# Spreading the token scales inside the second column pair of each SwiGLU stage, and other PSUM pools for that pair's tiles

## The chip, the cores and the metric

The kernel runs on one core of a Trainium2 chip. The metric is the device time of one launch in microseconds (us). Engines are called as in the profile: PE (TensorE matmul), PEld (its weight load), DVE (VectorE), ACT (ScalarE), POOL (GpSimd), SP (SyncE, which issues most transfers).

## What is computed

A decoder trunk of two layers over 512 tokens of width 1024, in float32. Each layer runs a half-step SwiGLU, a token mixer, a second half-step SwiGLU and a gated per-layer embedding. There are thus four SwiGLU stages, with a hidden width of 2816:

```python
def rms_norm(x, g, eps=NORM_EPS):
    y = x32 * lax.rsqrt(jnp.mean(x32 * x32, axis=-1, keepdims=True) + eps)
    return (y * g.astype(f32)).astype(x.dtype)
...
def swiglu(h, wg, wu, wd):
    return (jax.nn.silu(h @ wg) * (h @ wu)) @ wd
...
h = h + 0.5 * swiglu(rms_norm(h, norm_ffn_a[i]), ffn_a_wg[i], ffn_a_wu[i], ffn_a_wd[i])
```

## The kernel before

The activations stand transposed: eight tiles of 128 features by 512 tokens. A float32 product is made of three matmuls, since each operand is held as a high part and a remainder: `mm3` (L310) issues them. A weight block is loaded by SP, its high part is copied by ACT (L174) and the remainder is taken by DVE (L176). Such a pair is a piece; five slots hold pieces (`NHL`, L66), and `used` (L187) gives slots back and calls `pump`, which loads and splits what comes next.

The norm's gain is folded in before the matmul (`prep`, L350), but the scale of each token, 1/rms, is not: it is multiplied in later. `norm_stats` (L392) gets it: PE sums the squares into one column per token block (`token_rms`, L329), DVE makes the reciprocal root in eleven short instructions (L318 to L324), and `spread` (L333) turns the column into a full tile `Rt`: DVE puts it on a diagonal (L339), PE multiplies that with ones into the PSUM tile `rbc` (L344), DVE copies it out (L348).

`ffn` (L440) runs a list of steps. The hidden columns are taken in pairs of 128-column blocks. The first pair is computed plainly (`plain`, L444): for f = 0 and 1, 24 matmuls into a gate tile G (PSUM pool A) and 24 into an up tile U (pool B). Inside it stand `norm_stats` (L455), the building of four groups of combined inputs (`right`, L366, whose last instruction is DVE L382), and the plain pair's end, L459 to L463: gate times scale on DVE, Silu on ACT, up times gate on DVE, the high part on ACT, the remainder on DVE. Every other pair (`pair`, L465) uses a seven-product scheme: products in the order 0, 3, 4, 1, 5, 2, 6, each of 24 matmuls, gathered in three PSUM tiles X (pool A), Y (pool B) and Z (pool C). Products 3 to 6 read what `right` builds; product 0 and the plain products don't need L382. Product 2 goes to Z, the others to X and Y. L490, L492 and L495 copy partial sums out; L497, L499 and L501 put quarters of the result into O; product 6 goes on adding to X, so it follows L499. O shares its SBUF range with the scratch V of `right`.

PSUM has eight banks: pools A to D with two buffers each (L45). Pool C has no user in the plain pair. The order of instructions is not as written: the framework traces the program, then orders each engine's queue by program-order priority in a model of the run; each engine works its queue in order. A PSUM buffer is handed on when the last reader of its tile has run.

The four stages are called here a0, b0, a1, b1: first and second SwiGLU of layer 0, then of layer 1. `pair` for j = 1 follows `plain` at once and j = 2 follows that; the `down` steps (L514) come in from there.

Of the kernel before, what the change touches and what calls it, by code (L numbers as in the profile page):

```python
# [15 lines left out]
ALU = mybir.AluOpType  # L16
# [22 lines left out]
def trunk(ctx, tc, a, stop=None):  # L39
    nc = tc.nc  # L40
# [6 lines left out]
    def bank(tag, name="ps"):  # L47
        return psum.tile([P, NT], F32, tag=tag, name=name)
# [23 lines left out]
    O = fr[:, 0:2048].rearrange("p (f u n) -> p f u n", f=2, u=2)  # L72
    V = fr[:, 0:2048].rearrange("p (s n) -> p s n", s=8)
    aeb = [fr[:, 2048 + i * NT : 2048 + (i + 1) * NT] for i in range(3)]
    Rt = fr[:, 3584:4096]
# [9 lines left out]
    def sc(name="sc"):  # L85
        at = sc_at[scs[0] % (4 if wide[0] else 2)]
        scs[0] += 1
        return fr[:, at : at + NT]
# [98 lines left out]
    def used(*ps):  # L187
        for p in ps:
            hl_order.append(p.slot)
        pump()  # L190
# [27 lines left out]
    def done(u):  # L218
        used(*u.pieces)
# [90 lines left out]
    def mm3(ps, lh, ll, rh, rl, first, last):  # L310
        nc.tensor.matmul(ps, lh, rh, start=first, stop=False)  # L311
        nc.tensor.matmul(ps, lh, rl, start=False, stop=False)  # L312
        nc.tensor.matmul(ps, ll, rh, start=False, stop=last)  # L313
# [12 lines left out]
    def token_rms(sq, dim, eps, rcol):  # L326
        ps = bank("D", "ssum")
        for b in range(NB):
            nc.tensor.matmul(ps[:, b : b + 1], sq[:, b * P : (b + 1) * P], ones[:, 0:1],  # L329
                             start=True, stop=True)  # L330
        rsqrt_cols(rcol, ps[:, :NB], dim, eps, NB)

    def spread(rcol, dst, act=False):  # L333
        dg = sc("diag")
        if act:
            for b in range(NB):
                nc.scalar.activation(dg[:, b * P : (b + 1) * P], ident, AF.Copy, scale=rcol[:, b : b + 1])
        else:
            nc.vector.tensor_tensor(  # L339
            dg.rearrange("p (b n) -> p b n", n=P),  # L340
            ident[:, None, :].to_broadcast([P, NB, P]),
            rcol[:, :, None].to_broadcast([P, NB, P]), op=ALU.mult)
        ps = bank("D", "rbc")
        nc.tensor.matmul(ps, ones, dg, start=True, stop=True)  # L344
        if act:
            nc.scalar.activation(dst, ps, AF.Copy)
        else:
            nc.vector.tensor_copy(dst, ps)  # L348
# [43 lines left out]
    def norm_stats(want_row=True):  # L392
        rcol = small.tile([P, NB], F32, tag="rcol", name="rcol", bufs=2)
        token_rms(acc, DM, 1e-6, rcol)
        if not want_row:
            return rcol, None
        spread(rcol, Rt)
        return rcol, Rt
# [41 lines left out]
    def ffn(steps, me, nxt, side=None):  # L440

        state = {}

        def plain(ps):  # L444
            for f in range(2):
                G, U = bank("A", "G"), bank("B", "U")
                for c in range(KD):
                    w = [ps[2 * f + c % 2].part(s).rearrange("p (i n) -> p i n", i=4)[:, c // 2, :]
                         for s in range(2)]
                    for u, t in enumerate((G, U)):  # L450
                        us = slice(u * P, (u + 1) * P)
                        mm3(t, w[0][:, us], w[1][:, us], *plain_x[c], c == 0, c == KD - 1)
                used(*ps[2 * f : 2 * f + 2])
                if f == 0:
                    state["R"] = norm_stats()[1]  # L455
                for i in (2 * f, 2 * f + 1):
                    right(i, *me)
                g, u = (O[:, 1, k, :] for k in range(2)) if f else aeb[:2]
                nc.vector.tensor_tensor(g, G, state["R"], op=ALU.mult)  # L459
                nc.scalar.activation(g, g, AF.Silu)  # L460
                nc.vector.tensor_tensor(u, U, g, op=ALU.mult)
                nc.scalar.activation(hid[f], u, AF.Copy)
                nc.vector.tensor_tensor(hid[6 + f], u, hid[f].bitcast(F32), op=ALU.subtract)  # L463

        def pair(j, ps):  # L465
            X, Y, Z = bank("A", "X"), bank("B", "Y"), bank("C", "Z")
            k = [0]

            def product(op, out, start):
                p = ps[k[0]]  # L470
                k[0] += 1
                w = [p.part(s).rearrange("p (i n) -> p i n", i=4) for s in range(2)]
                for u in range(2):
                    o, us = out[:, u * 256 : (u + 1) * 256], slice(u * P, (u + 1) * P)
                    for i in range(4):
                        for n, (lw, r) in enumerate(((0, 0), (0, 1), (1, 0))):
                            nc.tensor.matmul(o, w[lw][:, i, us], xr[:, r, op, i, :],  # L477
                                             start=start and u == 0 and i == 0 and n == 0,
                                             stop=i == 3 and n == 2, skip_group_check=True)
                used(p)  # L480

            def quarter(f, t):
                return O[:, f, :, 256 * t : 256 * t + 256]

            def q2(t):
                return t.rearrange("p (u n) -> p u n", u=2)

            pa, pe, pb = aeb
            product(0, X, True)
            nc.scalar.activation(pa, X, AF.Copy, scale=-1.0)  # L490
            product(3, Y, True)
            nc.scalar.activation(pe, Y, AF.Copy, scale=-1.0)  # L492
            R = state["R"]
            product(4, X, False)
            nc.scalar.activation(pb, X, AF.Copy, scale=-1.0)  # L495
            product(1, Y, False)
            nc.vector.tensor_tensor(quarter(0, 0), q2(Y), q2(pb), op=ALU.add)  # L497
            product(5, X, False)
            nc.vector.tensor_tensor(quarter(1, 0), q2(X), q2(pe), op=ALU.add)  # L499
            product(2, Z, True)  # L500
            nc.vector.tensor_tensor(quarter(0, 1), q2(Z), q2(pa), op=ALU.add)  # L501
            product(6, X, False)
            nc.scalar.activation(quarter(1, 1), q2(X), AF.Copy)
            g, u = O[:, :, 0, :], O[:, :, 1, :]
            nc.vector.tensor_tensor(g, g, R[:, None, :].to_broadcast([P, 2, NT]), op=ALU.mult)
            nc.scalar.activation(g, g, AF.Silu)
            nc.vector.tensor_tensor(u, u, g, op=ALU.mult)
            s = next(s for s in range(4) if 2 * j < sum(SECTIONS[: s + 1]))
            t = 12 * (s % 2) + 2 * j - sum(SECTIONS[:s])
            h, lw = hidt[:, t : t + 2, :], hidt[:, t + 6 : t + 8, :]  # L510
            nc.scalar.activation(h, u, AF.Copy)
            nc.vector.tensor_tensor(lw, u, h.bitcast(F32), op=ALU.subtract)

        def down(s, u, unit):  # L514
            n = SECTIONS[s]
            for cc in range(2):
                c = 2 * u + cc
                ps = bank("D", "down")
                for f in range(n):
                    t = 12 * (s % 2) + f  # L520
                    mm3(ps, *unit.w(f, slice(cc * P, (cc + 1) * P)), hid[t], hid[t + 6],
                        f == 0, f == n - 1)
                t = sc("dt")
                nc.vector.tensor_tensor(t, ps, state["R"], op=ALU.mult)  # L524
                nc.vector.scalar_tensor_tensor(hT[c], t, 0.5, hT[c], op0=ALU.mult, op1=ALU.add)
                if s == len(SECTIONS) - 1:
                    prep(c, *nxt)
            done(unit)

        last = max(k for k, st in enumerate(steps) if st[0] == "dq")  # L530
        for k, st in enumerate(steps):
            if st[0] == "pl":
                plain(st[1])
            elif st[0] == "dq":
                pair(st[1], st[2])
            else:
                down(*st[1:])
                if k == last + 2 and side:
                    side()
# [16 lines left out]

    def ple(pt, ids, R, nxt):

        for c in range(KD):
# [5 lines left out]
            s = sc("sg")  # L565
            nc.vector.tensor_tensor(s, pg, R, op=ALU.mult)
            nc.scalar.activation(s, s, AF.Sigmoid)
# [512 lines left out]
    for l, d in enumerate(plans):  # L1080
        ffn(d["fa"], (l, 0), (l, 1))
        rcol, _ = norm_stats(False)
# [3 lines left out]
        if l == 0:  # L1086
            rcol, R = norm_stats()
            ple(box[0], d["ple"], R, (1, 0))
        else:
            rcol, _ = norm_stats(False)  # L1090
# [39 lines left out]
```

## Time and profile before

| | us |
|---|---|
| median of 3 runs | 2164.57 |
| lowest, highest | 2162.91, 2164.98 |
| profiled execution, its own time | 2164.67 |
| span of the profile | 2162.5 |
| mean granted TensorE clock | 0.975 of full |

The span runs from the first to the last recorded instruction. In the timeline a row is: start, duration, engine, line and operation, out<-in with the shape, how many instructions were merged, and in brackets the idle time of the engine before it and what ended that. Neighbouring rows of one engine overlap somewhat, since instructions are pipelined. A windows row is: from and to, its length, then the busy time of PE, PEld, DVE, ACT and POOL in it (with instruction counts), the granted TensorE clock as a share of full, the DMA share and GB/s.

### The profile page before, as it was taken

The page shows a single profiled execution, that of the slowest core. Times are in us where ns is not written, and L with a number is a line of the kernel's source. Part 1 is how long each engine was busy: PE and PEld are TensorE (multiplying, and loading weights), DVE is VectorE, ACT ScalarE, POOL GpSimd, SP SyncE. Part 2 cuts the span into 40 slices and gives each one's busy share as a digit, 9 for nine tenths or more (in the row PEclk, how much of TensorE's full clock was granted, in tenths as well). Part 3 has the DMA queues.
Part 4 walks back from the last instruction along what each step waited for, and adds up shares of the span by engine and source line. Part 5 has one row for each costly group of instructions (what it writes and reads, how often), then busy time and mean ns, then how long its engine had stood idle before and what let it go on. Part 6 is the DMA issues. An engine that isn't in the chain of part 4 may idle for free.

```text
span 2162.5 us, 33689 instructions
## 1 busy us (share of the span) xinstructions
PE 2048.6 (95%) x12995; PEld 1865.1 (86%) x12995; DVE 1663.7 (77%) x2666; ACT 1061.6 (49%) x1730; POOL 277.0 (13%) x249
## 2 busy tenths in 40 slices
PE   6999999988789799999999999999999979999998
PEld 4899998977677699999788999989989859999986
DVE  7787777688987797786677877766756688877765
ACT  5444444355455454444554444435755665444443
POOL 2000000533411000000310000014323110000011
PEclk8999999999899899999999999999999989999999
DMA  5333323222112133333233333332212213333331
GB/s 160 88 103 103 117 85 98 64 62 59 50 40 69 49 98 108 113 105 98 82 111 88 103 103 101 98 89 79 69 45 76 79 59 108 107 89 98 117 108 40
DMA packets 302048, 190.02 MB, mean 88 GB/s; under 512 B 14208, under 2 KB 292800, under 8 KB 301888
## 3 DMA queue, kind: packets, MB, share of 16 engines
q1 hardware_dynamic: 298592, 184.36, 28.9%
q10 hardware_dynamic: 2912, 2.46, 0.3%
q8 instruction: 102, 1.67, 0.3%
q0 software_dynamic: 384, 1.05, 0.2%
q14 instruction: 58, 0.48, 0.1%
HBM read 185.73 MB, written 2.10 MB: 87 GB/s over the span
## 4 chain that ended last, share of the span: by engine, by line
PE 84%; DVE 12%; issue 2%; DMA 1%; ACT 1%; SPq 0%; DVEq 0%; POOL 0%; ACTq 0%
PE X L477 21%; PE Y L477 10%; PE down L313 7%; PE down L311 7%; PE down L312 7%; PE Z L477 5%; PE proj L311 3%; PE proj L312 3%; PE proj L313 3%; PE pg L311 1%; PE pg L312 1%; PE pg L313 1%; PE pt L728 1%; PE outp L311 1%; PE outp L312 1%
## 5 line engine op out<-in xcount | busy, mean ns | idle before, releaser
L174 ACT ACTIVATE hl<-fr 128x1024 fp32r<-128x1024 f32 (+4 forms) x608 | 509.0, 856 | 651.6 <-PE X L477 285.3
L176 DVE TENSOR_TENSOR hl<-fr,hl 128x1024 fp32r<-128x1024 f32 (+2 forms) x473 | 530.0, 1128 | 164.6 <-ACT hl L174 161.1
L477 PE MATMUL X<-xr,hl 128*128 128x256 f32 x3840 | 484.8, 283 | 8.3 <-DVE fr L459 8.3
L477 PEld LDWEIGHTS X<-xr,hl 128*128 128x128 f32 x3840 | 474.7, 192 | 19.7 <-DVE fr L459 10.6
L311 PE MATMUL down<-hid,hl 128*128 128x512 f32 x704 | 273.6, 390 | 0.0
L313 PE MATMUL down<-hid,hl 128*128 128x512 f32 x704 | 273.4, 389 | 0.0
L312 PE MATMUL down<-hid,hl 128*128 128x512 f32 x704 | 273.4, 389 | 0.0
L477 PE MATMUL Y<-xr,hl 128*128 128x256 f32 x1920 | 238.3, 281 | 0.0
L477 PEld LDWEIGHTS Y<-xr,hl 128*128 128x128 f32 x1920 | 231.1, 189 | 0.0
L165 DVE TENSOR_TENSOR fr<-fr 128x1024 f32<-128x1024 f32 x160 | 197.8, 1237 | 25.4 <-DMA fr<-in_ffn_b_wu_dram 13.2
L176 POOL TENSOR_TENSOR hl<-fr,hl 128x512 fp32r<-128x512 f32 (+3 forms) x135 | 153.5, 1154 | 275.0 <-ACT hl L174 202.0
L311 PE MATMUL proj<-hl,xr 128*128 128x384 f32 (+2 forms) x512 | 169.8, 334 | 6.7 <-DVE fr L644 5.4
L312 PE MATMUL proj<-hl,xr 128*128 128x384 f32 (+2 forms) x512 | 169.9, 333 | 0.0
L313 PE MATMUL proj<-hl,xr 128*128 128x384 f32 (+2 forms) x512 | 169.4, 333 | 0.0
L313 PEld LDWEIGHTS down<-hid,hl 128*128 128x128 f32 x704 | 132.1, 188 | 26.4
L311 PEld LDWEIGHTS down<-hid,hl 128*128 128x128 f32 x704 | 132.2, 188 | 25.0
L312 PEld LDWEIGHTS down<-hid,hl 128*128 128x128 f32 x704 | 132.2, 188 | 24.8
L477 PE MATMUL Z<-xr,hl 128*128 128x256 f32 x960 | 132.7, 280 | 0.0
L477 PEld LDWEIGHTS Z<-xr,hl 128*128 128x128 f32 x960 | 121.3, 189 | 0.0
L652 POOL TENSOR_TENSOR fr<-fr 128x512 f32<-128x512 f32 (+1 forms) x72 | 91.0, 1271 | 224.1 <-DVE fr L644 111.9
L524 DVE TENSOR_TENSOR fr<-down,fr 128x512 f32<-128x512 f32 x128 | 87.8, 686 | 24.5 <-PE down L313 23.6
L311 PEld LDWEIGHTS proj<-hl,xr 128*128 128x128 f32 x512 | 97.5, 190 | 9.2 <-DVE fr L644 4.6
(227 smaller groups left out, 3144.2 us busy)
## 6 DMA issues: line engine op xcount, KB each, us to landing
fr<-in_ffn_a_wg_dram SPq DMA_DIRECT2D x88, 256.0 KB, 2.9
fr<-in_ffn_a_wu_dram SPq DMA_DIRECT2D x88, 256.0 KB, 3.4
fr<-in_ffn_b_wg_dram SPq DMA_DIRECT2D x88, 256.0 KB, 2.9
fr<-in_ffn_b_wu_dram SPq DMA_DIRECT2D x88, 256.0 KB, 3.3
fr<-in_ffn_a_wd_dram SPq DMA_DIRECT2D x48, 384.0 KB, 3.7
fr<-in_ffn_b_wd_dram SPq DMA_DIRECT2D x48, 384.0 KB, 3.9
fr<-in_odd_w_in_dram SPq DMA_DIRECT2D x96, 128.0 KB, 2.5
fr<-in_even_w_in_dram SPq DMA_DIRECT2D x56, 128.0 KB, 2.6
```

Source lines behind the costliest of these rows:

```text
L165: nc.vector.tensor_tensor(src, *(sums[x] if isinstance(x, int) else x.ap() for x in (a, b)), op=ALU.add)
L174: nc.scalar.activation(hi[:, s:e], src[:, s:e], AF.Copy)
L176: eng.tensor_tensor(lo[:, s:e], src[:, s:e], hi[:, s:e].bitcast(F32), op=ALU.subtract)
L311: nc.tensor.matmul(ps, lh, rh, start=first, stop=False)
L312: nc.tensor.matmul(ps, lh, rl, start=False, stop=False)
L313: nc.tensor.matmul(ps, ll, rh, start=False, stop=last)
L477: nc.tensor.matmul(o, w[lw][:, i, us], xr[:, r, op, i, :], start=start and u == 0 and i == 0 and n == 0, stop=i == 3 and n == 2, skip_grou ...
L524: nc.vector.tensor_tensor(t, ps, state["R"], op=ALU.mult)
L652: nc.gpsimd.tensor_tensor(dst, rv, tv, op=ALU.add)
L728: nc.tensor.transpose(ps[:, off : off + P], es[b][:, c * P : (c + 1) * P], ident)
```

## The change

In `ffn` alone. `plain` now calls only the column part of the norm (L455) and leaves both G and U tiles in PSUM. A new `plain_end`, called in the first `pair` (j = 1) behind product 4, spreads the scales and does the plain pair's end for f = 0 and 1; its scratch is O alone (before, for f = 0, the three tiles `aeb`, which `pair` uses for L490, L492, L495). In that pair X and Y come from pool C and Z from pool A; in later pairs they come from A, B and C as before.

```diff
                 if f == 0:
-                    state["R"] = norm_stats()[1]
+                    state["rcol"] = norm_stats(False)[0]
                 for i in (2 * f, 2 * f + 1):
                     right(i, *me)
-                g, u = (O[:, 1, k, :] for k in range(2)) if f else aeb[:2]
-                nc.vector.tensor_tensor(g, G, state["R"], op=ALU.mult)
+                state[f] = G, U
+
+        def plain_end():
+            spread(state["rcol"], Rt)
+            state["R"] = Rt
+            for f in range(2):
+                G, U = state[f]
+                g, u = (O[:, f, k, :] for k in range(2))
+                nc.vector.tensor_tensor(g, G, Rt, op=ALU.mult)
                 nc.scalar.activation(g, g, AF.Silu)
                 nc.vector.tensor_tensor(u, U, g, op=ALU.mult)
                 nc.scalar.activation(hid[f], u, AF.Copy)
                 nc.vector.tensor_tensor(hid[6 + f], u, hid[f].bitcast(F32), op=ALU.subtract)
 
         def pair(j, ps):
-            X, Y, Z = bank("A", "X"), bank("B", "Y"), bank("C", "Z")
+            X, Y, Z = (bank(t, n) for t, n in zip("CCA" if j == 1 else "ABC", "XYZ"))
...
             nc.scalar.activation(pe, Y, AF.Copy, scale=-1.0)
-            R = state["R"]
             product(4, X, False)
             nc.scalar.activation(pb, X, AF.Copy, scale=-1.0)
+            if j == 1:
+                plain_end()
+            R = state["R"]
             product(1, Y, False)
```

## Rows read from the trace of the kernel before

**Rows 1.** The page: busy time, share of span, instructions, by engine.

```profile
PE 2048.6 (95%) x12995; PEld 1865.1 (86%) x12995; DVE 1663.7 (77%) x2666; ACT 1061.6 (49%) x1730; POOL 277.0 (13%) x249
```

**Rows 2.** Waits of PE: us in total, times, longest.

```profile
PE rbc L344 <- DVE fr L339: 38.0, 4, 13.6
```

**Rows 3.** Timeline of PE, stage b1, plain pair's last work to pair two.

```profile
1758.05 0.95 PE L329 MATMUL ssum<-ones,fr 128*128 128x1 f32 x8
1770.81 2.08 PE L344 MATMUL rbc<-fr,ones 128*128 128x512 f32 x2 [11.81 <-DVE fr L339]
1774.39 4.39 PE L477 MATMUL X<-xr,hl 128*128 128x256 f32 x24 [1.51 <-DVE fr L459]
1778.62 2.88 PE L477 MATMUL Y<-xr,hl 128*128 128x256 f32 x24
...
1792.22 5.60 PE L477 MATMUL X<-xr,hl 128*128 128x256 f32 x48
```

**Rows 4.** Timeline of PE, stage a0.

```profile
59.25 5.15 PE L477 MATMUL X<-xr,hl 128*128 128x256 f32 x24 [1.60 <-DVE fr L459]
64.23 2.88 PE L477 MATMUL Y<-xr,hl 128*128 128x256 f32 x24
...
77.83 5.60 PE L477 MATMUL X<-xr,hl 128*128 128x256 f32 x48
```

**Rows 5.** Timeline of PE, stage b0.

```profile
733.66 5.49 PE L477 MATMUL X<-xr,hl 128*128 128x256 f32 x24 [1.51 <-DVE fr L459]
...
752.93 5.60 PE L477 MATMUL X<-xr,hl 128*128 128x256 f32 x48
```

**Rows 6.** Timeline of PE, stage a1 (last row cut off at 38 of 48).

```profile
1137.31 1.02 PE L344 MATMUL rbc<-fr,ones 128*128 128x512 f32 x2
1141.98 4.62 PE L477 MATMUL X<-xr,hl 128*128 128x256 f32 x24 [3.65 <-DVE fr L459]
1146.43 2.99 PE L477 MATMUL Y<-xr,hl 128*128 128x256 f32 x24
...
1160.57 4.64 PE L477 MATMUL X<-xr,hl 128*128 128x256 f32 x38
```

**Rows 7.** Windows, from the plain matmuls' end to the first `down` matmul.

```profile
42.04:96.87 54.83, 39.67 (x314) 38.16 (x315) 43.82 (x59) 27.56 (x33) 0.00 (x0) 0.84 0.29 87
718.26:771.97 53.71, 40.39 (x314) 38.81 (x315) 40.87 (x55) 24.98 (x30) 0.00 (x0) 0.84 0.30 88
1137.30:1180.00 42.70, 39.05 (x312) 38.22 (x311) 33.39 (x34) 22.62 (x27) 0.00 (x0) 0.96 0.34 99
1759.00:1811.26 52.26, 38.94 (x314) 37.37 (x315) 40.87 (x55) 24.97 (x30) 0.00 (x0) 0.84 0.31 90
```

**Rows 8.** Timeline of DVE: last L382 of stages a0, b0, a1, b1.

```profile
55.37 1.22 DVE L382 TENSOR_TENSOR xr<-fr,xr 128x1024 fp32r<-128x1024 f32 x1
...
723.25 1.22 DVE L382 TENSOR_TENSOR xr<-fr,xr 128x1024 fp32r<-128x1024 f32 x1
...
1136.01 1.22 DVE L382 TENSOR_TENSOR xr<-fr,xr 128x1024 fp32r<-128x1024 f32 x1
...
1763.99 1.22 DVE L382 TENSOR_TENSOR xr<-fr,xr 128x1024 fp32r<-128x1024 f32 x1
```

**Rows 9.** Timeline of DVE, stage b1: one split, then the scales and plain end.

```profile
1767.47 1.22 DVE L176 TENSOR_TENSOR hl<-fr,hl 128x1024 fp32r<-128x1024 f32 x1
1768.61 0.15 DVE L323 SCALAR_TENSOR_TENSOR rq<-rq,rv 128x4 f32<-128x4 f32 x1
...
1770.06 0.69 DVE L339 TENSOR_TENSOR fr<-ident,rcol 128x512 f32<-128x512 f32 x1
1772.92 0.69 DVE L348 COPY fr<-rbc 128x512 f32<-128x512 f32 x1 [2.17 <-PE rbc L344]
...
1776.42 1.36 DVE L463 TENSOR_TENSOR hid<-fr,hid 128x512 fp32r<-128x512 f32 x2
```

**Rows 10.** Timeline of ACT, stage b1.

```profile
1767.46 1.28 ACT L460 ACT_TABLE_LOAD   x1
```

## The prediction

> **What bounds the kernel now.** The page comes first: PE is busy 95% of the span, DVE 77% [rows 1], so time is to be had where PE stands still. The waits of PE come second. The longest is the spread's matmul behind DVE's diagonal: 38.0 us in four waits, the longest 13.6 [rows 2]. Third, the timeline of PE at the four places. In b1 the plain pair's matmuls and the column sums end at 1759.0; PE idles 11.81 us, runs the spread in 2.08, idles 1.51 behind the first gate eviction, and then runs the first product of pair one in 4.39 [rows 3], where a product takes 2.72 later on (48 matmuls in 5.44 net of the overlap of 0.16: half of it) [rows 3]. The second wait is there because X of pair one takes over the PSUM buffer of the first G. The slow product is PE coming back from its idle time at the lower of its two clock levels: the granted clock over the whole stretch is 0.84 [rows 7]. Stages a0 and b0 look alike [rows 4, 5]; in a1 there is no wait before the spread, only 3.65 us behind the eviction and a slow first product [rows 6].
>
> Fourth, the windows. Each begins where the plain matmuls (with the column sums) end, at 42.04, 718.26, 1137.30 and 1759.00, and ends at the first down. DVE works 43.82, 40.87, 33.39 and 40.87 us in them, so it idles 11.0, 12.8, 9.3 and 11.4 [rows 7]: **44.5 us together**, almost all after the plain end, since until then DVE is what all wait for. This is a ceiling: PE can be brought forward by what DVE has left and hardly more, or splits would have to be put off.
>
> **The change, part by part.** The instructions are the same in number and kind: one diagonal, one spread matmul, one copy, and the ten of the plain end, per stage. No transfer is issued or moved by hand; the loads behind `used` stand where they stood in the program, and may go out earlier as PE frees slots earlier. DMA is at 0.29 to 0.34 of its time there [rows 7], so I charge it nothing; its cover is that share, and without it each load would be late by its own length. SP's queue is passed by nothing new, and POOL has no work in these windows [rows 7].
>
> (1) X and Y of pair one lie in pool C, which is empty. Product 0 needs neither the scales nor L382, only its split piece, so it starts at the plain pair's end, inside what was idle time.
>
> (2) Product 3 needs the last L382. It ends at 55.37+1.22 = 56.6 in a0, 724.5 in b0, 1137.2 in a1 and 1765.2 in b1 [rows 8]. In a0 the diagonal (0.6) ran just ahead of it and now goes later, so I take 56.0. What is late next is therefore the combined inputs on DVE, not the scales.
>
> (3) From there six products (3, 4, 1, 5, 2, 6) at 2.72 follow, 16.3 us, and somewhere among them the spread's matmul, 1.0 us at full clock [rows 6]. Product 6 would end at 56.0+17.3 = 73.3 in a0, 741.8 in b0 and 1782.5 in b1. In a1, where L382 is done at the plain end, it is seven products of 2.83 (2.99 less overlap [rows 6]) and 1.0 from 1137.3: 1158.1. Before, product 6 ended 2.72 (a1 2.83) after the start of the long X row: 80.55, 755.65, 1163.4 and 1794.9 [rows 4, 5, 6, 3]. Brought forward: 7.2 + 13.9 + 5.3 + 12.4 = **38.8 us**.
>
> (4) The clock. In a0, b0 and b1 a gap remains, between product 0's end (about 44.8, 721.0, 1761.7) and L382: 11, 3.5 and 3.5 us. What a restart costs is shown by first products of 4.39 to 5.49 against 2.88 [rows 3 to 6]: 1.5 to 2.6 us; a1's 4.62 comes after an idle time of only 3.65 [rows 6], so the short gaps count too. Against this, the matmuls of product 3 on the first three input groups (18 of 24, about 2 us) can run inside the gap. Net between a gain of 2.0 and a loss of 2.6 for each; I take a loss of 0.5, nearer the middle, as which of them the ordering puts first is unknown: 1.5 us in all.
>
> (5) The new wait. Product 6 follows L499, which now writes into O behind the plain end's last instruction; Z waits for the first gate eviction, which is earlier in the same chain. Behind a waiting product 6 on PE's queue stands all of pair two. The chain, from the end of product 4 or of the diagonal (b1 today 1770.06+0.69 = 1770.8), whichever is later: the spread 1.0, then from the copy's start to L463's end 1776.42+1.36-1772.92 = 4.9 [rows 9], L499 0.7, and splits that DVE takes between: one costs 1.14 (start to start [rows 9]) and three are due by then (products 0, 3 and 4 hand back their slots), 3.4. Sum 10.0. In b1 product 4 ends at 1765.2+5.4 = 1770.6, so L499 ends at 1780.8; product 6 is due at 1782.5-2.72 = 1779.8: 1.0 late. The same working gives 0.9 in b0, 0.8 in a0 and 0.6 in a1. The diagonal itself now ranks behind those splits, which adds 0 to 3.4 in b0 and b1, where the column is ready latest; I take half. The load of Silu's table on ACT, 1.28 [rows 10], had idle time to hide in and would lengthen the chain if it doesn't: 0 to 1.3 a stage, taken as 0, since it can run while ACT waits for the gate. Sum: 3.3 + 3.4 = 6.7, with bounds of 0 and 3.3 + 6.8 + 5.2 = 15.
>
> (6) After pair one DVE has less lead. I use 38.8-1.5-6.7 = 30.6 of its 44.5 us of idle time, so I charge nothing more; the cover is the remaining 14.
>
> **Sum.** The profiled execution took 2164.67 (span 2162.5 and 2.2 around it), 0.1 above the median of 2164.57. 2164.7-30.6 = 2134.1; I forecast **2133**, leaving a microsecond for the diagonal's move in the lighter stages.
>
> **Rivals.** (A) DVE becomes the bound. For it: in each window it works 74 to 80% already [rows 7], and between ready pieces it waits for ACT, which waits for slots. Against it: five slots let the splits slip. If only a third of its idle time can be used, the gain is 15 and the time 2150; with half, 2142.
>
> (B) Slower. The place is the chain of (5): what the old order did with high rank, it now does behind the splits. If DVE also splits all five slots for pair two first, with the four sums that those need (of about the same length, an estimate), that is nine more instructions of 1.14 ahead of the plain end, 10.3 us, and product 6 waits for all of it. The kernel turns slower once the plain end slips by more than 30.6/4 = 7.7 us per stage beyond (5); with 10.3 in each of four stages it is 2133+41 = 2174. For it: four PSUM buffers are held through two more products, and Z has no other place. Against it: slots for pair two come free only as the products of pair one end, so DVE can't run so far ahead; and the only waits on a bank now, 1.51 to 3.65 us before pair one [rows 3 to 6], go away, as pool C stands empty meanwhile. The Trainium skill, "PSUM — Partial Sum Buffer", section "Summary: rules for kernel authors", advises to evacuate promptly because PSUM is tight; here four of the eight banks are held longer, and by that rule the outcome would be this rival's 2174 rather than 2133. No row of the kernel before shows a wait that bears the rule out in pair one.
>
> (C) It does little. The ordering may keep the spread's matmul ahead of all of pair one in PE's queue; then PE waits for the diagonal as before, and only the idle time between the spread and X goes, 1.60+1.51+1.51+3.65 = 8.3 us [rows 3 to 6], less the 6.7 of (5): 2163, within 0.2%. Against it: in program order the spread now stands behind product 4.
>
> (D) More. If the first three groups of product 3 fill the gaps, no restart costs anything and the plain end never holds PE, it is 38.8+6.0 = 44.8, which is also DVE's ceiling: 2120.
>
> **How the numbers follow.** A measurement of this kernel can tell about 0.2%, 4.3 us. Chances: my forecast (2124 to 2139) 0.60; (A) (2139 to 2155) 0.20; (D) 0.09; (C) 0.05; (B) 0.06. The range takes my own case, (D)'s end with 3 us for a reordering elsewhere, and (A) to a third of the idle time: 2117 to 2150. Outside lie (B), (C) and the tail of (A): under 0.2. Faster by over 0.2%: 0.60+0.20+0.09 = 0.89; within: 0.05; slower: 0.06.
>
> **What would show it.** Right: X of pair one starts within a microsecond of the last plain matmul; PE's longest wait there names L382 and lasts about 3 us in b0 and b1 and longer in a0; the wait for the diagonal is gone from the waits of PE; product 6 starts some 1 to 3 us after L499's inputs from PE are there; DVE's idle time in the four windows falls from 44.5 to about 14. Wrong: PE stands at the spread's matmul or at product 6 for more than 5 us, pairs two and three wait for splits, or the windows end less than 4 us earlier than before.

## The result, and the profile after

The changed kernel takes **2136.72 us** (median of 4 runs, 2135.36 to 2137.97) against 2163.74 for the kernel before on the same chip (4 runs, 2161.49 to 2164.98): ratio 0.9875, 95% interval 0.986 to 0.989. That is 27.0 us less; the sum of the prediction came to 30.6. The profiled execution took 2136.96 us, with a span of 2135.2.

Line numbers move: in the changed kernel products are L484 (before L477), the plain end is L466 to L470 (before L459 to L463), and L497, L499, L501 are the copies before numbered L490, L492, L495. L318 to L348 and L382 keep their numbers.

The page's first part, and the waits of PE (total, times, longest), of the changed kernel:

```profile
PE 2047.3 (96%) x12995; PEld 1865.2 (87%) x12995; DVE 1660.9 (78%) x2666; ACT 1059.6 (50%) x1730; POOL 276.6 (13%) x249
```

```profile
PE rbc L344 <- DVE fr L339: 9.8, 4, 5.8
...
PE Z L484 <- DVE fr L466: 5.6, 2, 2.8
```

The busy times are within 3 us of those of [rows 1], as no work was taken away. The 38.0 us behind the diagonal [rows 2] have become 9.8, and two new waits of 2.8 stand behind the plain end's first gate eviction; three short ones, 3.0 us together, are behind L497, the copy of product 0's X. No row for L382 is among the long ones.

Windows of the four stages, changed kernel, from the plain matmuls' end to the first `down` matmul as in [rows 7]:

```profile
42.20:90.90 48.70, 40.45 (x314) 38.70 (x313) 43.54 (x58) 26.80 (x33) 0.00 (x0) 0.86 0.34 98
711.15:756.40 45.25, 39.87 (x310) 38.27 (x309) 38.87 (x52) 24.65 (x30) 0.00 (x0) 0.92 0.36 105
1121.95:1159.10 37.15, 37.15 (x314) 36.67 (x313) 32.84 (x34) 22.33 (x27) 0.00 (x0) 1.00 0.39 114
1738.80:1783.90 45.10, 39.74 (x309) 38.19 (x308) 38.82 (x52) 24.59 (x30) 0.00 (x0) 0.92 0.35 105
sum 176.20, PE 157.21 PEld 151.82 DVE 154.08 ACT 98.36 POOL 0.00; mean PE 39.30 PEld 37.96 DVE 38.52 ACT 24.59 POOL 0.00
```

Against [rows 7] they are shorter by 6.1 (a0), 8.5 (b0), 5.6 (a1) and 7.2 (b1): 27.3 us, as much as the difference of the spans (2162.5 - 2135.2). In b0 and b1, however, they hold 310 and 309 matmuls instead of 314, since five of product 0 ran before the window began, and the stretch ahead of the window is 0.8 us longer for it. Counted from the stage's first matmul to its first `down` matmul, the stages are shorter by 6.1, 7.7, 5.6 and 6.4 us, 25.8 together. Most of what is left lies in the first mixer, which the change does not touch: from the end of a0's `down` to b0's first plain matmul it took 309.7 us before and 307.8 now. Why is not shown. Stage a1 has no idle PE left: busy 37.15 of 37.15, at the full clock.

Timeline of PE in b0, changed kernel, from the last plain work to pair two (b1 has the same rows, its waits within 0.02):

```profile
710.92 2.32 PE L484 MATMUL X<-xr,hl 128*128 128x256 f32 x19
713.08 1.30 PE L484 MATMUL Y<-xr,hl 128*128 128x256 f32 x10
715.04 1.43 PE L484 MATMUL X<-xr,hl 128*128 128x256 f32 x10 [0.67 <-ACT fr L497]
716.78 1.87 PE L484 MATMUL Y<-xr,hl 128*128 128x256 f32 x14 [0.32 <-DVE xr L382]
718.49 1.75 PE L484 MATMUL X<-xr,hl 128*128 128x256 f32 x14
720.22 3.09 PE L484 MATMUL Y<-xr,hl 128*128 128x256 f32 x24
723.15 2.99 PE L484 MATMUL X<-xr,hl 128*128 128x256 f32 x24
727.72 1.12 PE L344 MATMUL rbc<-fr,ones 128*128 128x512 f32 x2 [1.58 <-DVE fr L339]
731.66 5.49 PE L484 MATMUL Z<-xr,hl 128*128 128x256 f32 x24 [2.82 <-DVE fr L466]
736.95 5.99 PE L484 MATMUL X<-xr,hl 128*128 128x256 f32 x48
```

The kernel before had in this place in b0, as in b1 [rows 3]:

```profile
730.07 2.08 PE L344 MATMUL rbc<-fr,ones 128*128 128x512 f32 x2 [11.81 <-DVE fr L339]
```

Where 11.81 us of idle time stood, products 0, 3, 4, 1 and 5 now run. Matmuls of products 3 and 4 (Y x10, X x10) go ahead on the input groups that are ready, so the wait for the last L382 is 0.32. What holds PE is the spread (1.58), then Z: product 2 needs the first gate's PSUM buffer, which L466 has not yet read (2.82). Then Z runs at half speed, 5.49 for 24 matmuls against 2.88.

In a0 the order on PE is another: nine matmuls each of products 3 and 4 go ahead, and the spread is queued in front of the rest of them.

```profile
46.31 0.38 PE L484 MATMUL Y<-xr,hl 128*128 128x256 f32 x1 [0.75 <-ACT xr L381]
48.35 1.86 PE L484 MATMUL X<-xr,hl 128*128 128x256 f32 x7 [1.66 <-ACT fr L497]
...
57.04 2.04 PE L344 MATMUL rbc<-fr,ones 128*128 128x512 f32 x2 [5.84 <-DVE fr L339]
```

Timeline of DVE in the same place, changed kernel:

```profile
711.43 0.15 DVE L318 TENSOR_SCALAR rv<-ssum 128x4 f32<-128x4 f32 x1
...
715.44 0.16 DVE L323 SCALAR_TENSOR_TENSOR rq<-rq,rv 128x4 f32<-128x4 f32 x1
715.51 1.22 DVE L382 TENSOR_TENSOR xr<-fr,xr 128x1024 fp32r<-128x1024 f32 x1
716.65 1.22 DVE L165 TENSOR_TENSOR fr<-fr 128x1024 f32<-128x1024 f32 x1
...
718.92 0.16 DVE L324 SCALAR_TENSOR_TENSOR rcol<-rq,rcol 128x4 f32<-128x4 f32 x1
...
726.78 0.15 DVE L324 SCALAR_TENSOR_TENSOR rcol<-rq,rcol 128x4 f32<-128x4 f32 x1
726.97 0.69 DVE L339 TENSOR_TENSOR fr<-ident,rcol 128x512 f32<-128x512 f32 x1
...
729.19 0.68 DVE L348 COPY fr<-rbc 128x512 f32<-128x512 f32 x1
...
730.92 1.28 DVE L466 TENSOR_TENSOR fr<-G,fr 128x512 f32<-128x512 f32 x2
```

The column is eleven instructions of 0.15, each needing the one before. Between nearly every two stand one to three instructions of 1.2 us that were ready: the remainders L176, the sums L165 of weight blocks that some pieces need, and the last L382. So the column lasts from 711.43 to 726.93, 15.5 us, and the diagonal, the spread and the plain end all stand behind it. In the kernel before the column was interleaved too, but less, and the diagonal started 10.0 us after the column's first instruction:

```profile
719.30 0.15 DVE L318 TENSOR_SCALAR rv<-ssum 128x4 f32<-128x4 f32 x1
...
729.32 0.69 DVE L339 TENSOR_TENSOR fr<-ident,rcol 128x512 f32<-128x512 f32 x1
```

The column starts at the same place in both, 29.2 us after the first plain matmul of the stage.

### The profile page after: what moved, and what is told of

The parts are those of the page before. It is cut to its first block, busy times and chain, and to the rows that moved or that the text cites. A ratio compares the mean times of both kernels' runs of the same rounds, so it can differ in the third digit from the quotient of the medians.

```text
span 2135.2 us, 33697 instructions
## 1 busy us (share of the span) xinstructions
PE 2047.3 (96%) x12995; PEld 1865.2 (87%) x12995; DVE 1660.9 (78%) x2666; ACT 1059.6 (50%) x1730; POOL 276.6 (13%) x249
## 4 chain that ended last, share of the span: by engine, by line
PE 84%; DVE 11%; ACT 2%; DMA 1%; issue 1%; SPq 0%; DVEq 0%; POOL 0%; ACTq 0%
PE X L484 20%; PE Y L484 10%; PE down L312 7%; PE down L311 7%; PE down L313 7%; PE Z L484 6%; PE proj L311 3%; PE proj L312 3%; PE proj L313 3%; PE pg L311 1%; PE pg L312 1%; PE pg L313 1%; PE pt L737 1%; PE outp L311 1%; PE outp L312 1%
## 5 line engine op out<-in xcount | busy, mean ns | idle before, releaser
L176 DVE TENSOR_TENSOR hl<-fr,hl 128x1024 fp32r<-128x1024 f32 (+2 forms) x473 | 530.6, 1130 | 143.5 <-ACT hl L174 137.7
L484 PE MATMUL X<-xr,hl 128*128 128x256 f32 x3840 | 481.4, 281 | 3.0 <-ACT fr L497 3.0
L484 PEld LDWEIGHTS X<-xr,hl 128*128 128x128 f32 x3840 | 470.9, 190 | 11.2 <-ACT fr L497 3.6
L484 PE MATMUL Y<-xr,hl 128*128 128x256 f32 x1920 | 242.4, 282 | 1.4 <-ACT xr L381 0.8
L484 PEld LDWEIGHTS Y<-xr,hl 128*128 128x128 f32 x1920 | 233.0, 190 | 2.8 <-DVE xr L382 1.0
L165 DVE TENSOR_TENSOR fr<-fr 128x1024 f32<-128x1024 f32 x160 | 197.5, 1236 | 28.3 <-DMA fr<-in_ffn_a_wu_dram 13.4
L176 POOL TENSOR_TENSOR hl<-fr,hl 128x512 fp32r<-128x512 f32 (+3 forms) x135 | 152.8, 1149 | 274.9 <-ACT hl L174 188.3
L484 PE MATMUL Z<-xr,hl 128*128 128x256 f32 x960 | 136.2, 288 | 5.6 <-DVE fr L466 5.6
L484 PEld LDWEIGHTS Z<-xr,hl 128*128 128x128 f32 x960 | 125.4, 196 | 7.3 <-DVE fr L466 7.3
```

What stands on the lines that cost most here:

```text
L165: nc.vector.tensor_tensor(src, *(sums[x] if isinstance(x, int) else x.ap() for x in (a, b)), op=ALU.add)
L176: eng.tensor_tensor(lo[:, s:e], src[:, s:e], hi[:, s:e].bitcast(F32), op=ALU.subtract)
L484: nc.tensor.matmul(o, w[lw][:, i, us], xr[:, r, op, i, :], start=start and u == 0 and i == 0 and n == 0, stop=i == 3 and n == 2, skip_grou ...
```

## The experiments

All ratios are to the kernel before on the same chip (medians 2163.00, 2164.08 and 2164.34 in three sets of runs).

| run | base, edit | us | ratio, 95% interval |
|---|---|---|---|
| e1 | before, pools alone | 2148.27 | 0.9932 (0.9917 to 0.9946) |
| e2 | changed, old pools | 2164.50 | 1.0005 (0.9995 to 1.0014) |
| e3 | changed, Z in pool D | 2131.94 | 0.9860 (0.9844 to 0.9876) |
| e4 | changed, plain end behind product 0 | 2135.77 | 0.9877 (0.9862 to 0.9892) |
| e5 | changed, one step for the column | 2121.08 | 0.9803 (0.9790 to 0.9817) |
| e6 | changed, column first | 2116.85 | 0.9784 (0.9770 to 0.9797) |
| e7 | e6 and Z in pool D | 2115.49 | 0.9777 (0.9763 to 0.9790) |
| e8 | e7, spread first too | 2118.69 | 0.9793 (0.9780 to 0.9807) |
| e9 | before, column first | 2158.53 | 0.9973 (0.9962 to 0.9983) |
| e10 | e1, column first | 2142.04 | 0.9899 (0.9884 to 0.9914) |

### The two halves of the change: e1 and e2

e1 gives the kernel before the new pools and leaves the plain end where it was:

```diff
-            X, Y, Z = bank("A", "X"), bank("B", "Y"), bank("C", "Z")
+            X, Y, Z = (bank(t, n) for t, n in zip("CCA" if j == 1 else "ABC", "XYZ"))
```

> The kernel before with one edit: X and Y of pair one in pool C, Z in pool A; spread and plain end stay in the plain pair. Theory (both parts are needed): products 0 and 3 can start, since no PSUM buffer of G is in their way, but product 4 needs the copy L490 into the scratch that the plain end for f = 0 still uses, so PE waits there for the plain end; about half of the gain of 27 us is left, 2150 (2144 to 2157). Rival 1 (the bank was all that mattered): 2137 or less. Rival 2 (the order was all that mattered): 2162 to 2166.

e2 is the changed kernel with the old pools:

```diff
-            X, Y, Z = (bank(t, n) for t, n in zip("CCA" if j == 1 else "ABC", "XYZ"))
+            X, Y, Z = (bank(t, n) for t, n in zip("ABC", "XYZ"))
```

> The changed kernel with one edit: X, Y and Z of pair one in pools A, B, C as before; spread and plain end stay behind product 4 in program order. Theory: X has to take over the buffer of the first G, so no product of pair one starts before the first gate eviction; PE idles there as before, 10 us and more in a0, b0 and b1, and the time is 2158 to 2170. Rival 2 (the order alone brings the gain): 2137 to 2142.

e1 took 2148.27, e2 2164.50. The waits of PE in e1:

```profile
PE rbc L344 <- DVE fr L339: 17.9, 4, 6.3
PE Y L477 <- DVE xr L382: 8.1, 3, 3.3
```

and in e2:

```profile
PE rbc L344 <- DVE fr L339: 38.0, 4, 13.6
PE X L484 <- DVE fr L466: 8.3, 4, 3.7
```

where the kernel before has, beside the same 38.0 [rows 2]:

```profile
PE X L477 <- DVE fr L459: 8.3, 4, 3.6
```

The pools alone bring 14.7 us, the later plain end alone nothing measurable, both 27. Both times lie in the ranges given. In e2 the first product has no buffer until the plain end has run, so the waits are those of before to a tenth, whatever the program's order says. In e1 products 0 and 3 start at once. Then PE stands at the spread, which is queued next (5.29 us in b0), and at product 2, which waits for the first gate's buffer (1.60 in b0); product 4 runs only behind these. That product 4 has to wait for its copy L490, whose scratch the plain end uses (for f = 0 it takes two of the three tiles `aeb`), was the reason that I had given for it; L490 does run only at 731.75 in b0, behind the plain end's use of that scratch, but no wait of PE in b0 names it. The move of the plain end pays only once there is a free buffer to work in.

### The bank of Z, and the plain end's rank: e3 and e4

e3 takes Z of pair one from pool D (`"CCD"` in place of `"CCA"`). e4 puts the plain end behind product 0:

```diff
             nc.scalar.activation(pa, X, AF.Copy, scale=-1.0)
+            if j == 1:
+                plain_end()
+            R = state["R"]
             product(3, Y, True)
...
             nc.scalar.activation(pb, X, AF.Copy, scale=-1.0)
-            if j == 1:
-                plain_end()
-            R = state["R"]
             product(1, Y, False)
```

> The changed kernel with one edit: Z of pair one in pool D in place of A, so that it doesn't wait for the first gate eviction (2.8 us in b0 and b1 in the changed kernel's trace). Theory (the plain end's chain through DVE holds PE, and the bank is only the first place where it shows): the wait moves to product 6, behind L508, which follows the plain end in O; at most 1 us per stage b is won, 2133 to 2138. Rival (holding the bank is the cost): wait and slow restart of Z both go, 2.8 + 2.7 in each of two stages, 2124 to 2128.

> The changed kernel with one edit: the plain end stands behind product 0 in program order, ahead of the splits that products 3 and 4 call for. Theory (the spread and the plain end are late because DVE takes splits first): in b0 and b1 two splits or more, 2.3 us and more, come off the wait of PE for diagonal and eviction, and a part of the slow restart; 2127 to 2134. Rival (DVE has too much to do in either order): what the plain end wins, the pieces of products 5, 2 and 6 lose; within 3 us of 2137, or slower.

e3 took 2131.94: 4.8 less than the changed kernel, or 4.0 when each is set against the kernel before in its own set of runs. That is between the two ranges: holding the bank costs more than my theory had it, and less than its rival. The timeline of PE in b0 of e3 shows Z without a wait and at nearly full speed; smaller waits come up behind it in pair two, the longest at pair two's own Z:

```profile
726.46 1.13 PE L344 MATMUL rbc<-fr,ones 128*128 128x512 f32 x2 [1.69 <-DVE fr L339]
727.03 3.39 PE L484 MATMUL Z<-xr,hl 128*128 128x256 f32 x24
730.40 3.00 PE L484 MATMUL X<-xr,hl 128*128 128x256 f32 x24
...
738.88 2.97 PE L484 MATMUL Z<-xr,hl 128*128 128x256 f32 x24 [1.66 <-DVE fr L506]
```

e4 took 2135.77, within a microsecond of the changed kernel: here my first theory of the lateness, that the plain end's place in the program ranks it behind the splits, **fell**. The rival's time, within 3 us of 2137, is what came. The diagonal's wait (9.9 in four) and Z's (5.6 in two) are the same. DVE's order in b0 was the same as well: what is late is the column, and its place in the program had not been touched.

### The column: e5, e6, e7 and e8

e5 shortens the column from eleven instructions to five: one refinement step in place of three for the SwiGLU scales (`for _ in range(steps)`, with 1 from `ffn`). It computes those scales less exactly.

> The changed kernel with one edit: the reciprocal root of the SwiGLU stages' token scale takes one refinement step in place of three (six of the eleven short DVE instructions left out, so the scale is less exact). The six weigh 6 x 0.1 = 0.6 us of DVE by themselves. Theory (the column comes late because DVE takes a split of 1.14 us between any two of these dependent instructions): the diagonal comes some 4 us earlier in b0 and b1, its wait of 1.58 goes and most of the 2.82 of Z with the slow restart: 2122 to 2131. Rival (DVE's total decides, the order of its work doesn't): 2135 to 2138.

e6 does the same arithmetic as the changed kernel and only alters the order: what `used` issues (the loads and splits of the next pieces) for f = 1 and for products 0, 3 and 4 of pair one is queued behind the column's last instruction.

```diff
-                used(*ps[2 * f : 2 * f + 2])
+                with tc.issue_after(state["col"].ins) if f else ExitStack():
+                    used(*ps[2 * f : 2 * f + 2])
                 if f == 0:
                     state["rcol"] = norm_stats(False)[0]
+                    state["col"] = last_rsqrt[0]
...
-                used(p)
+                with tc.issue_after(state["col"].ins) if j == 1 and op in (0, 3, 4) else ExitStack():
+                    used(p)
```

> The changed kernel with only DVE's order edited: the splits called for by the plain pair's second half and by products 0, 3 and 4 are queued behind the last instruction of the reciprocal root, so nothing comes between its instructions. Same arithmetic as the changed kernel. Theory (the column's dependent instructions interleaved with splits are what PE waits for): column 4 us or more earlier, 2122 to 2132. Rival (DVE's total decides, or the splits put off are now late): 2135 or more, with PE waiting for pieces.

e5 took 2121.08, e6 2116.85: both below the ranges that I had set, e5 by 1 us and e6 by 5. Timeline of DVE in b0 of e6 (L326 is the column's last line, L341 the diagonal, L350 the copy):

```profile
703.75 0.15 DVE L320 TENSOR_SCALAR rv<-ssum 128x4 f32<-128x4 f32 x1
...
707.99 0.16 DVE L326 SCALAR_TENSOR_TENSOR rcol<-rq,rcol 128x4 f32<-128x4 f32 x1
708.07 2.36 DVE L165 TENSOR_TENSOR fr<-fr 128x1024 f32<-128x1024 f32 x2
```

and of PE (L488 are the products, L470 the first gate eviction):

```profile
712.22 1.13 PE L346 MATMUL rbc<-fr,ones 128*128 128x512 f32 x2 [0.56 <-DVE fr L341]
...
720.23 2.99 PE L488 MATMUL Z<-xr,hl 128*128 128x256 f32 x24 [0.46 <-DVE fr L470]
```

The column takes 4.4 us (703.75 to 708.15) where it took 15.5, and Z's wait falls from 2.82 to 0.46, with no slow matmuls behind it. The windows of the same four stages in e6:

```profile
41.70:86.80 45.10, 40.52 (x316) 38.38 (x314) 42.78 (x57) 26.82 (x32) 0.00 (x0) 0.92 0.41 117
703.40:742.10 38.70, 36.95 (x310) 35.31 (x310) 37.90 (x51) 24.55 (x30) 0.00 (x0) 1.00 0.43 127
1109.00:1146.30 37.30, 37.30 (x315) 36.82 (x314) 33.92 (x35) 22.44 (x27) 0.00 (x0) 1.00 0.49 142
1724.60:1764.20 39.60, 37.95 (x311) 36.32 (x310) 38.87 (x52) 25.37 (x30) 0.00 (x0) 1.00 0.45 133
```

Their sum is 160.7 against 176.2: 15.5 of the 19.7 us between the two spans (2135.2 and 2115.5), most of it in b0 and b1. The other 4.2 lie outside the windows, 3.6 of them in the first mixer, from the end of a0's `down` to b0's first plain matmul (307.8 to 304.2 us); why the order there came out better I did not try. Every run with the column first has this stretch at 302.3 to 305.0 us and every other run at 305.8 to 309.7, so that part of e6's gain goes with the edit, but not through the waits told here.

DVE works 153.5 of the 160.7 us in these windows. Of the 44.5 us of idle time that the prediction gave as the ceiling, e6 has used 42.8 (203.5 - 160.7), so by that measure only 1.7 is left there to win by order alone.

e6's edit moves more than the column: the last combined inputs (L382, in e6 L384) no longer stand behind those splits either, and end 2.3 us earlier in b0 and 4.8 in a0, counted from the stage's first matmul. e5 tells the two apart, as it leaves them where they were in b0 and 1.4 us later in a0. In b0 and b1 it shortens the stage by 6.9 and 6.8 us (first matmul to first `down`), e6 by 6.6 and 5.7: there the column is what counted. In a0 e5 has the diagonal 9.9 us earlier and wins only 0.8, while e6 wins 3.7: there the combined inputs were late, not the column.

e7 is e6 with Z in pool D; e8 is e7 with the diagonal, the spread and the copy ahead of the splits as well (the whole of `norm_stats` back in its old place, and `used` behind the diagonal).

> Both edits: Z of pair one in pool D and the column's instructions kept together. Theory (column late and bank held are two waits one behind the other in b0 and b1): together 2120 to 2129, faster than either alone. Rival (one chain, the shorter column makes the bank not matter): the same as the one with the column first, within 2 us.

> As the one before, but the spread stands in the plain pair in program order as in the kernel before, and the splits are queued behind its diagonal in place of the column's last instruction; the plain end stays behind product 4. Theory: the diagonal is one to three splits earlier than with the column alone, 2118 to 2128. Rival (too many splits put off): PE waits for pieces of products 3 and 4, slower than the one before.

e7 took 2115.49, within 2 us of e6, as its rival said: with the column early, the first gate's buffer is free almost when Z wants it, and of the gain of e3 only 1.4 us is left. e8 took 2118.69, inside the range given, but 3 us more than e7. The wait is not the one that its rival named, for pieces of products 3 and 4: Z of pair two stands 5.1 us in two behind L509, an eviction of quarters into O, so putting still more ahead of the splits gave nothing. e6 and e7 are the fastest here, some 20 us below the changed kernel and 47 to 49 below the one before.

### Was the column's order alone the fault? e9 and e10

e9 applies e6's edit to the kernel before, e10 to e1 (the new pools, the plain end early in the program).

> The kernel before with one edit: the column of the token scales is queued ahead of the splits of the second feature half and of products 0, 3 and 4 on VectorE, as in the run with the column first; the plain pair's end and its eight banks stay as they were. Theory (the column's order and the change gain from different waits): the first product still waits for the diagonal, the spread, the copy and the first gate eviction, because the plain pair holds the banks until then, and only the column's stretch gets shorter, about 5 us in each of the b stages, 6 in a0 and 0 to 2 in a1: 2148 us (2142 to 2154). Rival (the column's order alone was the fault, and neither the moved end nor the pools are needed): 2115 to 2125 us.

> The kernel before with the pools of the change and the column first, but with the plain pair's end where it stood in the program of before, ahead of the second pair's products. Theory: products 0 and 3 start at once in the idle pool, and product 4, whose group copies stand behind the plain pair's end in the order of the program, waits for it: 2125 to 2140 us. Rival (with the column first the spread comes so early that it does not matter where the plain pair's end stands): within 2 us of 2117 us.

e9 took 2158.53, 5.8 us less than before and 4.5 above the range given, and e10 2142.04, 2 us above its range. Neither comes near e6: the rival of each is refuted, and the gain in my own theory was too large for both. Timeline of PE in b0 of e9 (products L481, first gate eviction L463):

```profile
718.24 2.07 PE L346 MATMUL rbc<-fr,ones 128*128 128x512 f32 x2 [8.40 <-DVE fr L341]
724.97 5.49 PE L481 MATMUL X<-xr,hl 128*128 128x256 f32 x24 [4.65 <-DVE fr L463]
```

Beside the kernel before in b0 the wait for the diagonal shrank from 11.81 to 8.40, but that for the eviction rose from 1.51 [rows 5] to 4.65, since the splits that were put off now come between spread, copy and eviction: 3.4 won, 3.1 given back. The windows of e9 sum to 205.7 us against 203.5 in [rows 7]; its gain lies in the first mixer (309.7 us in before, 302.3 in e9). In e10 the same stretch reads:

```profile
716.95 2.08 PE L346 MATMUL rbc<-fr,ones 128*128 128x512 f32 x2 [3.60 <-DVE fr L341]
723.92 5.46 PE L481 MATMUL Z<-xr,hl 128*128 128x256 f32 x24 [4.89 <-DVE fr L463]
```

with product 4 queued behind Z. From e10 to e6 only the plain end's move differs, with its scratch: 25 us. From e1 to e10 the column's order brings 6, and 4.1 of that is the first mixer's. In the four stages the column's order thus costs 2.2 us with the old pools and the early plain end (e9), wins 2.6 with the new pools (e10) and 15.5 once the plain end is moved too (e6). So the two work together: the change provides work for PE to do meanwhile, and only then does an earlier column shorten what PE still waits for.

## Why the prediction was right, and where its size was off

The sign and the range held, and so did the main part of the mechanism: products of pair one now run where PE stood still, because their buffers are free. 2136.7 lies 3.7 above the 2133 forecast, inside the forecast's own 2124 to 2139. What PE waits for next was named rightly for a0 alone. Point by point:

- **(1)** right. X starts at 41.99 in a0, 0.2 after the last plain matmul's start. In b0 and b1 five of its matmuls run even before the plain pair's last ones, which I had not expected.
- **(2)** has the times right and the conclusion right for a0 alone. In b0 the last L382 ends 5.3 us after the column's first instruction (716.73 - 711.43), against 5.2 before. But the wait for it is 0.32 there, and it is the scales that are late in b0 and b1, not the combined inputs. In a0, where the inputs are late, L382 slipped to 58.37 (46.0 after the stage's start of 12.4, against 44.3 before), since more DVE work stands ahead of it.
- **(3)** holds as the sum without waits.
- **(4)** was charged in the wrong place. In b0 and b1 nothing restarted at product 3: products 3 and 4 together ran 20 matmuls in the gap, near the best case of my bounds, and the waits were 0.67 and 0.32. The slow product is Z instead, 2.6 above 2.88.
- **(5)** is the term that failed, in b0 and b1. I let the diagonal rank 0 to 3.4 us later and took half. It started 15.5 us after the column's first instruction in b0 (726.97 - 711.43) against 10.0 before (729.32 - 719.30): **5.5 later, beyond my bound**, and 5.6 in b1. I had counted the splits that might stand ahead of the diagonal, but not those that get between the column's eleven dependent instructions; the rows of a split just ahead of L323 and of the diagonal behind it [rows 9] showed the pattern, and I read only its end. Then I had product 6 wait, and dismissed Z as "earlier in the same chain". Product 2 is queued ahead of product 6, so it was Z that stopped PE; when it was done, product 6 had no wait.
- **(6)** right in charging nothing: no split holds up pair two in b0 or b1. The cover was mis-sized: DVE idles 22.1 us in the four windows (176.20 - 154.08), where I had 14.
- **The sum** gave 2134.1. The last microsecond, down to 2133, has no row behind it: a later diagonal would lengthen the time.

By stage, net of (4) and (5), the forecast was 5.9 (a0), 10.8 (b0), 4.7 (a1) and 9.2 (b1); measured from the stage's first matmul to the end of product 6 it is 6.1, 7.7, 5.6 and 6.4. The two b stages lack 5.9 us together, a1 gives 0.9 back and a0 0.2, and the first mixer adds 1.9 that the prediction did not have. That the total came within a few us is thus luck in part. So is a0's 6.1 against 5.9: L382 ended 2.3 us later than (2) took it, and from there to the end of product 6 it took 16.2 us where (3) to (5) make 18.6.

Of what was to be seen, X and the windows came as said, and DVE's idle time fell by half, not to 14. Three signs did not come: the wait for the diagonal is not gone, the longest wait of PE there names it or Z and not L382, and product 6 does not wait. One sign of being wrong did come: in a0 PE stands 5.84 us at the spread, above the 5 that I had set. The spread's matmul is queued ahead of the last matmuls of products 3 and 4 there, so the wait bears another name. The diagonal was ready at 56.89 and L382 at 58.37, so most of those products would have waited anyway.

The rivals: (A) is refuted for the changed kernel, since e6 runs 20 us faster with the same DVE work; e6 itself comes near to it, with DVE at work 153.5 of 160.7 us. The share of DVE that (A) starts from is 76 to 80% by [rows 7], not 74 to 80%. (C) is refuted as what the change does, though e2 shows its outcome where the pools stay, and a0 has its order in part. (B) had the right neighbourhood and too high a price: the chain does stand behind splits, but it costs two waits of 2.82 and a slow product each, not 10.3 in every stage. Its argument for, that Z has no other place, and its argument against, that the waits on a bank go away, are both wrong: Z could go to pool D (e3), and in pool A it waits for a bank. The Trainium skill, "PSUM — Partial Sum Buffer", "Summary: rules for kernel authors", which advises prompt evacuation, has its trace here in Z's 2.82 us, and e3 shows 4 to 5 us for the two stages; the change as a whole, which holds four buffers longer, still gained 27. (D), 2120, is about what e6 reached: what I gave up there as unlikely needed only another order on DVE.

## What to carry to other kernels

Moving work off the path pays only where the engine has somewhere to put the next result: look for the free PSUM buffer first, then move the eviction. When a chain of short dependent instructions shares an in-order queue with long ready ones, price the chain with a long one or more between every two links, here 15.5 us for eleven instructions instead of 4.4, and keep it together once it is what others wait for. A queue edit that shortens one wait can lengthen the next by as much (e9): follow the chain to the first instruction that PE truly needs.

## What was not expected of the hardware

What a pause cost in clock did not follow from its own length alone. Windows of the changed kernel, two of b0 and one of a0 (the last field but two is the granted clock):

```profile
715.04:726.00 10.96, 10.64 (x86) 10.20 (x86) 10.58 (x17) 5.21 (x6) 0.00 (x0) 1.00 0.45 129
731.66:736.95 5.29, 5.29 (x25) 5.29 (x26) 4.33 (x7) 2.44 (x4) 0.00 (x0) 0.50 0.00 0
48.35:50.00 1.65, 1.65 (x7) 1.60 (x8) 1.65 (x4) 0.00 (x0) 0.00 (x0) 0.50 0.00 0
```

and one of b0 in e3, behind a single wait of 1.69:

```profile
727.03:730.40 3.37, 3.37 (x26) 2.94 (x24) 3.37 (x5) 0.07 (x1) 0.00 (x0) 1.00 0.48 141
```

In b0, after waits of 0.67 and 0.32 us, PE went on at 1.00, its upper level of 2.4 GHz, and in e3 it did so after 1.69. After 1.58 and 2.82 us of idle time with only the spread between them, it ran the whole of Z at 0.50, the lower level of 1.2 GHz. But in a0 waits of 0.75 and 1.66 with a single matmul between them were enough for 0.50. Two waits close together thus cost what one as long as the longer of them did not. I had charged a loss to every gap; in b0 the short ones cost only their own length, and the pair of 1.58 and 2.82 cost 2.6 us in Z on top of it, nearly as much as the longer wait itself.
